# Output projections in two Strassen groups: additions to the accumulators moved, and VectorE's fixed order made longer

## The chip, the cores and the metric

The kernel runs on one core of a Trainium2 chip. The metric is the device time of one execution in microseconds (us), as the median of several executions. The engines are named as in the profile: PE is TensorE (matrix products), DVE VectorE, ACT ScalarE, POOL GpSimd, SP SyncE (which issues DMAs).

## What is computed

A decoder trunk of two layers on one sequence of 1024 tokens with 1024 features, all in float32. Layer 0 mixes tokens by sliding-window attention, layer 1 by a chunked spatial gating unit (SGU); after each comes a gated feed-forward block (FFN) with a short convolution. Each of the four blocks stands between two RMS norms.

```python
for i in range(DEPTH):
    h = rms_norm(x, norm_mix_pre[i])
    h = sliding_window_attention(h, ...) if i % 2 == 0 else chunked_sgu(h, ...)
    x = x + rms_norm(h, norm_mix_post[i])
    h = conv_gated_ffn(rms_norm(x, norm_ffn_pre[i]), ...)
    x = x + rms_norm(h, norm_ffn_post[i])

def conv_gated_ffn(h, w_in, conv_w, conv_b, w_out):
    g, u = jnp.split(h @ w_in, 2, axis=-1)
    ...
    return (jax.nn.gelu(g) * u) @ w_out
```

The change concerns the last product of a block, `... @ w_out`, in three of the four: both FFNs (2816 rows of `w_out`) and the SGU (3072 rows).

## The kernel before

**Products.** A float32 product is made of three passes over rounded operands: each operand is split into a high and a low half (`split`, line 806: a copy on ACT at line 808, then a subtraction on DVE, by the helper at line 602), and PE computes high by high, high by low and low by high (`passes`). A DVE or ACT instruction takes a tile of 128 x 512.

**Output projection.** `out_phase_` (line 911 on) is run three times: FFN of layer 0, SGU, FFN of layer 1. `w_out`'s rows come in chunks of 128: 22 in an FFN, 24 in the SGU. Pairs of chunks are multiplied by Strassen's scheme in Winograd's form, seven products in place of eight, over quarters of the 1024 x 1024 output: accumulators `c[i, j]`, four tiles of 128 x 512 each, i and j from zero (`c[1, 0]` is the lower left quarter). The first group g1 has six pairs (products P1, P2, P6, P5, P7, P3, P4), the second group g2 has n2 pairs, four in an FFN and five in the SGU, in the order Q1, Q2, Q6, Q5, Q3, Q7, Q4. The last two chunks are multiplied directly: `chunk` splits them in Q1 (tiles `ohl`), and `part` adds their products to the same PSUM banks as Q2, Q3, Q7 or Q4 use.

**Steps.** A product has one step for each pair: `prepare` splits its two operands into `osum` tiles, `go` does the product's extra work `what(g)` for this pair and then 12 matmuls (line 880). In the last step of a product, `more` is called for each of its four banks as that is done, and `done` for all four. Steps are numbered through: 0 to 41 are g1; in an FFN Q1 is 42 to 45, Q2 46 to 49, Q6 50 to 53, Q5 54 to 57, Q3 58 to 61, Q7 62 to 65, Q4 66 to 69. In the SGU each has five: Q2 is 47 to 51, Q6 52 to 56, Q4 ends with 76.

**Extra work in g2.** `sums2` (in Q2's steps) does three DVE subtractions on blocks that Q6 and Q5 read, `sums4` (in Q5's) one DVE addition to a block that Q3 reads. `c11` (Q2's `more`; the names of these functions count from one, so it completes the quarter `c[0, 0]`) calls `part`: an addition from the bank to the accumulator on DVE (line 262), the square with its sum on ACT (line 269, output `junk`), a multiplication by the gain on DVE (line 270); line 275 begins the norm. Q1's result is copied to four tiles `u` (the list `ww`). `u2` (Q6's `done`) adds Q6's banks to them and the sums to `c[1, 0]`; `u4` (Q5's `done`) subtracts and adds the result to `c[0, 1]` and `c[1, 1]`. `c12`, `c22` and `c21` complete and normalise the other parts.

**Order.** `run_products` (line 890) writes out the order: step i's `go` comes after the `prepare` of step i + 2, from step 38 on of step i + 3. For steps 0 to 29 (`5 * NPAIR`) DVE takes its instructions in just that order; from there on a scheduler orders DVE's queue, as it does the other engines' throughout. The `osum` tiles come from a pool of eight (`wp`), of which two of the `ohl` pairs take four from Q1 on. The `mm` banks are four; Q1, Q5 and Q7 use them, while Q6 and Q3 use the banks `ob` and `tb`.

Of the kernel before, what the change touches and what calls it, by code (L numbers as in the profile page):

```python
# [37 lines left out]
def trunk_kernel(  # L38
# [113 lines left out]
    def half_of(i):  # L152
        return slice(i * HALF, (i + 1) * HALF)
# [447 lines left out]
    def sub_(out, a, b, eng=None):  # L601
        (eng or nc.vector).tensor_tensor(out=out, in0=a, in1=b, op=ALU.subtract)  # L602

    def add_(out, a, b, eng=None):
        (eng or nc.vector).tensor_tensor(out=out, in0=a, in1=b, op=ALU.add)  # L605
# [182 lines left out]
    NPAIR = 6  # L788
# [100 lines left out]

    def run_products(products):  # L890

        steps = [s for p in products for s in p.steps()]
        n = 0

        def go(i0, i1):
            nonlocal n
            for i in range(i0, i1):
                while n < min(i + AHEAD[i >= 7 * NPAIR - 4] + 1, len(steps)):
                    steps[n][0]()
                    n += 1  # L900
                steps[i][1]()

        with tc.manual_schedule(engines={mybir.EngineType.DVE}):
            go(0, 5 * NPAIR)
        go(5 * NPAIR, len(steps))

    def out_phase(nchunk, ad, w_out, make_sub):
        with tc.tile_pool(name="junkp", bufs=2) as junkp:
            return out_phase_(nchunk, ad, w_out, make_sub, junkp)

    def out_phase_(nchunk, ad, w_out, make_sub, junkp):
# [10 lines left out]
        def w_block(j0):  # L922
            return lambda g, k, i: w_out[tok(j0 + 2 * g + k), half_of(i)]
# [21 lines left out]
        c = {(i, j): [sub.acc[4 * i + t][:, half_of(j)] for t in range(4)] for i in range(2) for j in range(2)}  # L945
# [13 lines left out]
        def add_to(dst):  # L959
            def f(b):  # L960
                for t in range(4):
                    add_(dst[t], b[t], dst[t])
            return f

        def less(dst, src):

            def f(b):
                for t in range(4):
                    sub_(dst[t], b[t], src[t])
            return f  # L970

        def from_(dst, src):

            def f(b):
                for t in range(4):
                    sub_(dst[t], src[t], b[t])
            return f

        def both(*fs):
            def f(b):  # L980
                for x in fs:
                    x(b)
            return f

        def same(p):
            return lambda: p.banks
# [8 lines left out]
        P5 = Product(g1, "P5", four0, both(g1.late, g1.sums4), less(c[0, 1], c[1, 0]))  # L995
        P7 = Product(g1, "P7", four1, None, both(from_(c[1, 1], c[0, 1]), lambda b: load((0, 1))))
        P3 = Product(g1, "P3", four0, None, add_to(c[0, 1]))
# [4 lines left out]
        g2 = Group(n2, [(xnp, "xn")] * 4 + [(work, "work")] * (n2 - 4), w_block(2 * NPAIR))  # L1002
# [5 lines left out]
        def load(parts):  # L1008
            for item in list(todo):
                what, k, i, g, part = item  # L1010
                free = [p for p in parts if spare[p] and p in (part, 2)]
                if not free:
                    continue
                todo.remove(item)
                t = spare[free[0]].pop(0)
                j = 2 * NPAIR + 2 * g + k
                if what == "A":
                    nc.sync.dma_start(out=t, in_=ad[j][:, half_of(i)])
                    g2.A[g][i, k] = t
                else:  # L1020
                    nc.sync.dma_start(out=t, in_=w_out[tok(j), half_of(i)])
                    g2.B[g][k, i] = t
# [24 lines left out]
        ww = []  # L1047
# [7 lines left out]
        def u2(b):  # L1055
            for t in range(4):
                add_(ww[t], b[t], ww[t])
                add_(c[1, 0][t], ww[t], c[1, 0][t])

        def u4(b):  # L1060
            for t in range(4):
                sub_(ww[t], b[t], ww[t])
                add_(c[0, 1][t], ww[t], c[0, 1][t])
                add_(c[1, 1][t], ww[t], c[1, 1][t])

        def c11(t, b):
            part(t, 0, b)
# [14 lines left out]
        Q1 = Product(g2, "P1", four0, both(g2.sums1, chunk), u1)  # L1082
        Q2 = Product(g2, "P2", same(Q1), g2.sums2, more=c11, first=False)
        Q6 = Product(g2, "P6", four1, g2.sums3, u2)
        Q5 = Product(g2, "P5", four0, g2.sums4, u4)
        Q3 = Product(g2, "P3", four1, more=c12)
        Q7 = Product(g2, "P7", four0, None, c22)
        Q4 = Product(g2, "P4", same(Q7), more=c21, first=False)
        run_products(seq + [Q1, Q2, Q6, Q5, Q3, Q7, Q4])
        return sub.h  # L1090

# [376 lines left out]
```

## Time and profile before

| | |
|---|---|
| median of three executions | 2475.07 us (2474.7 to 2475.67) |
| the profiled execution | 2475.61 us, of which span 2473.9 us |
| PE busy | 2414.4 us |
| DVE busy | 1851.3 us |
| ACT busy | 1052.4 us |
| matmuls of line 880 in the chain that ended last | 17% of the span |

The span is the time from the first instruction in the profile to the last; the rest of an execution lies around it. Busy time of PE includes matmuls that run at a lower clock. In a timeline each row is an instruction, or some alike in a row (x4), with its start, its time, its line and in brackets the idle time of the engine just before it and what ended that. One instruction's time overlaps the next one's start a little, so costs are read from start to start.

### The profile page before, as it was taken

How to read it: one execution, taken by the hardware profiler on the slowest of the kernel's cores; microseconds unless marked ns; L12 is line 12 of the kernel's file. 1: busy time of each engine (PE TensorE's matmuls, PEld its weight loads, DVE VectorE, ACT ScalarE, POOL GpSimd, SP SyncE). 2: the span in 40 equal slices, each digit the busy share in tenths (PEclk: the TensorE clock that was granted, in tenths of full speed). 3: DMA queues.
4: the chain of work that ended last, by engine and by line, in shares of the span. 5: the costliest groups of instructions: out<-in, count | busy, mean ns of one | idle time of the engine just before them, and what ended most of it. 6: DMA issues, size and time to landing. Idle time of an engine off the chain costs nothing.

```text
span 2473.9 us, 33879 instructions
## 1 busy us (share of the span) xinstructions
PE 2414.4 (98%) x12488; PEld 2029.6 (82%) x12488; DVE 1851.3 (75%) x3224; ACT 1052.4 (43%) x1957; POOL 341.8 (14%) x442
## 2 busy tenths in 40 slices
PE   9999989999999999999999999999999999999997
PEld 8777778888887787789998888788797888887886
DVE  5766799767767887886667776787887767767877
ACT  4654565333333444443333333444453333334443
POOL 1000010000000111100027777202110000001011
PEclk9999999999999999999999999999999999999999
DMA  7322142222224952433334444974222222238642
GB/s 238 65 47 56 44 154 69 77 87 92 69 94 154 260 156 69 153 107 99 94 97 148 135 141 150 295 220 81 94 95 85 68 94 86 76 103 259 192 86 102
DMA packets 269943, 296.34 MB, mean 120 GB/s; under 512 B 30447, under 2 KB 195665, under 8 KB 269778
## 3 DMA queue, kind: packets, MB, share of 16 engines
q1 hardware_dynamic: 257106, 271.11, 34.2%
q0 software_dynamic: 12672, 23.07, 5.7%
q8 instruction: 98, 1.61, 0.3%
q14 instruction: 67, 0.55, 0.1%
HBM read 211.29 MB, written 65.01 MB: 112 GB/s over the span
## 4 chain that ended last, share of the span: by engine, by line
PE 84%; DVE 10%; DMA 3%; issue 2%; ACT 1%; POOL 0%; SPq 0%; DVEq 0%; POOLq 0%; ACTq 0%
PE mm L748 27%; PE ob L748 11%; PE mm L880 11%; PE mm L148 7%; PE mm L1286 6%; PE ob L880 3%; PE ob L259 3%; PE tb L880 3%; PE ob L1286 2%; DVE osum L602 2%; PE tb L1416 2%; DMA raw<-ad 2%; PE mm L259 1%; DMA raw<-in_ffn_w_out 1%; PE tb L473 1%
## 5 line engine op out<-in xcount | busy, mean ns | idle before, releaser
L748 PE MATMUL mm<-T,wsum 128*128 128x512 f32 x2496 | 597.4, 392 | 5.4 <-ACT wsum L710 4.2
L748 PEld LDWEIGHTS mm<-T,wsum 128*128 128x128 f32 x2496 | 468.3, 189 | 105.8 <-ACT wsum L710 6.0
L880 PE MATMUL mm<-osum 128*128 128x512 f32 x1644 | 390.1, 391 | 8.1 <-ACT osum L808 4.4
L880 PEld LDWEIGHTS mm<-osum 128*128 128x128 f32 x1644 | 306.6, 188 | 76.0 <-DVE osum L602 5.8
L808 ACT CAST osum<-raw 128x512 fp32r<-128x512 f32 x372 | 215.8, 619 | 305.2 <-PE mm L880 103.7
L602 DVE TENSOR_TENSOR osum<-raw,osum 128x512 fp32r<-128x512 f32 x372 | 242.9, 690 | 84.2 <-ACT osum L808 84.0
L748 PE MATMUL ob<-hhi,wsum 128*128 128x512 f32 x864 | 287.3, 393 | 0.1
L710 ACT CAST wsum<-sums 128x512 fp32r<-128x512 f32 x208 | 127.7, 621 | 292.8 <-DVE sums L602 164.1
L1401 POOL TENSOR_SCALAR vn<-vn,mv,rv 128x128 f32<-128x128 f32 x192 | 193.3, 1018 | 73.9 <-DMA vn<-vd 26.2
L602 DVE TENSOR_TENSOR wsum<-sums,wsum 128x512 fp32r<-128x512 f32 x208 | 142.8, 690 | 68.0 <-ACT wsum L710 67.5
L748 PEld LDWEIGHTS ob<-hhi,wsum 128*128 128x128 f32 x864 | 161.7, 188 | 35.7 <-ACT wsum L710 3.4
L748 PE MATMUL ob<-hlo,wsum 128*128 128x512 f32 x432 | 168.7, 390 | 0.0
L710 ACT CAST wsum<-raw 128x512 fp32r<-128x512 f32 x156 | 96.5, 620 | 163.7 <-PE mm L748 140.3
L605 DVE TENSOR_TENSOR pu<-mm,pu 128x512 f32<-128x512 f32 x110 | 75.7, 688 | 105.4 <-PE mm L748 105.3
L880 PE MATMUL ob<-osum 128*128 128x512 f32 x480 | 133.8, 393 | 13.8 <-DVE osum L602 13.8
L148 PE MATMUL mm<-hhi,whi 128*128 128x256 f32 (+1 forms) x416 | 136.0, 329 | 0.7 <-ACT hhi L211 0.7
L148 PE MATMUL mm<-hlo,whi 128*128 128x256 f32 (+1 forms) x416 | 135.7, 327 | 0.0
L148 PE MATMUL mm<-hhi,wlo 128*128 128x256 f32 (+1 forms) x416 | 134.6, 325 | 0.2 <-DVE wlo L125 0.2
L880 PE MATMUL tb<-osum 128*128 128x512 f32 x480 | 132.5, 389 | 0.0
L748 PE MATMUL mm<-hhi,wsum 128*128 128x512 f32 x384 | 126.7, 391 | 0.0
L1116 DVE SCALAR_TENSOR_TENSOR cv<-gs,cw,cv 128x1024 f32<-128x1024 f32 (+1 forms) x100 | 115.7, 1157 | 14.1 <-issue 8.3
L880 PEld LDWEIGHTS ob<-osum 128*128 128x128 f32 x480 | 88.9, 188 | 38.0 <-DVE osum L602 20.2
(257 smaller groups left out, 4526.6 us busy)
## 6 DMA issues: line engine op xcount, KB each, us to landing
raw<-in_ffn_w_in SPq DMA_DIRECT2D x88, 512.0 KB, 4.0
raw<-ad SPq DMA_DIRECT2D x80, 256.0 KB, 5.4
raw<-in_ffn_w_out SPq DMA_DIRECT2D x80, 256.0 KB, 5.7
ad<-cv SPq DMA_DIRECT2D x38, 512.0 KB, 3.2
raw<-in_sgu_w_in SPq DMA_DIRECT2D x28, 512.0 KB, 4.4
xs<-xt SPq DMA_DIRECT2D x24, 512.0 KB, 2.6
vn<-vd SPq DMA_DIRECT2D x48, 256.0 KB, 3.2
ads<-ut SPq DMA_DIRECT2D x24, 512.0 KB, 3.1
```

Of the source, the lines that this page charges most:

```text
L148: nc.tensor.matmul(ps[:, cs], a[:, k, :], b[:, k, cs], start=n == 0, stop=n == 3 * KC - 1)
L259: nc.tensor.matmul(ps, a, b[:, half_of(nh)], start=n == 0 and not begun, stop=n == end, skip_group_check=begun)
L602: (eng or nc.vector).tensor_tensor(out=out, in0=a, in1=b, op=ALU.subtract)
L605: (eng or nc.vector).tensor_tensor(out=out, in0=a, in1=b, op=ALU.add)
L710: nc.scalar.copy(out=t[:, 0], in_=src)
L748: nc.tensor.matmul(bank, x, y, start=first and n == 0, stop=n == 3 * H4 - 1, skip_group_check=True)
L808: nc.scalar.copy(out=t[:, 0], in_=src)
L880: nc.tensor.matmul(self.banks[t], u, v, start=self.first and g == 0 and m == 0, stop=last and self.more is None and m == 2, skip_group_che ...
L1116: nc.vector.scalar_tensor_tensor(out=cv, in0=gs[j][:, k + t0:k + t0 + n], scalar=tap_w(k, j), in1=cv, op0=ALU.mult, op1=ALU.add)
L1286: nc.tensor.matmul(bank[r][:, q * NQ:(q + 1) * NQ], x, y, start=first and q == 0 and m == 0, stop=m == 3 * H4 - 1, skip_group_check=True)
L1401: nc.gpsimd.tensor_scalar(out=vn[:, t, :], in0=vn[:, t, :], scalar1=mv[:, tt, 0:1], scalar2=rv[:, tt:tt + 1], op0=ALU.subtract, op1=ALU.mult)
L1416: nc.tensor.matmul(sv[:, t, :], vn[:, t, :], gws[(j + i) // 3][0], start=True, stop=True)
```

## The change

It does two things. First, `u2` and `u4` keep only the four additions or subtractions on the `u` tiles. What they added to the accumulators, a new function `plus_u(i, j)` does, one tile a step, in the first four steps of a later product: `c[1, 0]` in Q5's (ahead of sums4), `c[0, 1]` in Q3's, `c[1, 1]` in Q7's. Second, DVE's fixed order now reaches to step 61 of an FFN's 70 steps and step 66 of the SGU's 77: all but the last step of Q3, and Q7 and Q4.

```diff
+        fixed = len(steps) - 2 * products[-1].group.n - 1
         with tc.manual_schedule(engines={mybir.EngineType.DVE}):
-            go(0, 5 * NPAIR)
-        go(5 * NPAIR, len(steps))
+            go(0, fixed)
+        go(fixed, len(steps))
...
         def u2(b):
             for t in range(4):
                 add_(ww[t], b[t], ww[t])
-                add_(c[1, 0][t], ww[t], c[1, 0][t])
 
         def u4(b):
             for t in range(4):
                 sub_(ww[t], b[t], ww[t])
-                add_(c[0, 1][t], ww[t], c[0, 1][t])
-                add_(c[1, 1][t], ww[t], c[1, 1][t])
+
+        def plus_u(i, j):
+
+            return lambda t: add_(c[i, j][t], ww[t], c[i, j][t]) if t < 4 else None
...
-        Q5 = Product(g2, "P5", four0, g2.sums4, u4)
-        Q3 = Product(g2, "P3", four1, more=c12)
-        Q7 = Product(g2, "P7", four0, None, c22)
+        Q5 = Product(g2, "P5", four0, both(plus_u(1, 0), g2.sums4), u4)
+        Q3 = Product(g2, "P3", four1, plus_u(0, 1), more=c12)
+        Q7 = Product(g2, "P7", four0, plus_u(1, 1), c22)
```

What this does to the order of the engines' queues is shown for the FFN of layer 0; the numbers in names tell tiles apart. Lines behind 889 are two or three higher in the changed kernel.

**VectorE, from Q2 to Q6.** `acc_7333` to `acc_7336` are the tiles on which c11 works; `osum_8386` and `osum_8389` are the two splits for Q6's first step, `osum_8408` and `osum_8411` for its second. Before:

```order
L602 TENSOR_TENSOR osum_8386<-raw1_7275,osum_8386 128x512
L602 TENSOR_TENSOR osum_8389<-sums_7341,osum_8389 128x512
L262 TENSOR_TENSOR acc_7333<-mm_8256,acc_7333 128x512
L270 TENSOR_TENSOR acc_7333<-acc_7333,gpost_7263 128x512
L275 TENSOR_SCALAR ms_8759<-ss2_8451 128x1
L262 TENSOR_TENSOR acc_7334<-mm_8257,acc_7334 128x512
L262 TENSOR_TENSOR acc_7335<-mm_8258,acc_7335 128x512
L270 TENSOR_TENSOR acc_7334<-acc_7334,gpost_7263 128x512
L275 TENSOR_SCALAR ms_8790<-ss2_8465 128x1
L602 TENSOR_TENSOR osum_8408<-raw1_7275,osum_8408 128x512
L602 TENSOR_TENSOR osum_8411<-sums_7342,osum_8411 128x512
```

In the changed kernel, where the three subtractions of sums2 for Q2's last step and the beginning of c11 stand (`osum_8429` and `osum_8432` are the splits for Q6's third step):

```order
L602 TENSOR_TENSOR osum_8429<-raw1_7275,osum_8429 128x512
L602 TENSOR_TENSOR osum_8432<-sums_7343,osum_8432 128x512
L602 TENSOR_TENSOR sums_7344<-raw1_7277 128x512
L602 TENSOR_TENSOR raw1_7277<-raw1_7275,raw1_7277 128x512
L602 TENSOR_TENSOR raw1_7275<-sums_7344,raw1_7275 128x512
L262 TENSOR_TENSOR acc_7333<-mm_8255,acc_7333 128x512
L270 TENSOR_TENSOR acc_7333<-acc_7333,gpost_7263 128x512
```

and c11's end, with the splits for Q6's last step (`osum_8495`, `osum_8498`) and for Q5's first (`osum_8518`, `osum_8521`):

```order
L270 TENSOR_TENSOR acc_7335<-acc_7335,gpost_7263 128x512
L262 TENSOR_TENSOR acc_7336<-mm_8258,acc_7336 128x512
L275 TENSOR_SCALAR ms_8829<-ss2_8478 128x1
L270 TENSOR_TENSOR acc_7336<-acc_7336,gpost_7263 128x512
L602 TENSOR_TENSOR osum_8495<-raw1_7275,osum_8495 128x512
L602 TENSOR_TENSOR osum_8498<-sums_7344,osum_8498 128x512
L602 TENSOR_TENSOR osum_8518<-sums_7341,osum_8518 128x512
L602 TENSOR_TENSOR osum_8521<-raw1_7275,osum_8521 128x512
```

Before, c11's instructions stood around the splits for Q6's second step, and sums2's subtractions were far ahead (with P4 and Q1). Now they stand behind the splits for Q6's third step and all subtractions, and ahead of those for its last.

**ScalarE, at the same place.** The squares of c11's tiles are the four lines 269. Before (the copies are for Q6's steps, two each, and Q5's first, `osum_8519` and `osum_8522`):

```order
L269 ACTIVATE junk_8443,ss2_8451<-acc_7333 128x512
L269 ACTIVATE junk_8457,ss2_8465<-acc_7334 128x512
L808 CAST osum_8408<-raw1_7275 128x512
L808 CAST osum_8411<-sums_7342 128x512
L269 ACTIVATE junk_8471,ss2_8479<-acc_7335 128x512
L269 ACTIVATE junk_8485,ss2_8493<-acc_7336 128x512
L808 CAST osum_8430<-raw1_7275 128x512
L808 CAST osum_8433<-sums_7343 128x512
L808 CAST osum_8496<-raw1_7275 128x512
L808 CAST osum_8499<-sums_7344 128x512
L808 CAST osum_8519<-sums_7341 128x512
L808 CAST osum_8522<-raw1_7275 128x512
```

In the changed kernel (`osum_8518` and `osum_8521` are for Q5's first step):

```order
L808 CAST osum_8429<-raw1_7275 128x512
L808 CAST osum_8432<-sums_7343 128x512
L808 CAST osum_8495<-raw1_7275 128x512
L808 CAST osum_8498<-sums_7344 128x512
L808 CAST osum_8518<-sums_7341 128x512
L808 CAST osum_8521<-raw1_7275 128x512
L269 ACTIVATE junk_8442,ss2_8450<-acc_7333 128x512
L269 ACTIVATE junk_8456,ss2_8464<-acc_7334 128x512
L269 ACTIVATE junk_8470,ss2_8478<-acc_7335 128x512
L269 ACTIVATE junk_8484,ss2_8492<-acc_7336 128x512
L808 CAST osum_8537<-sums_7342 128x512
```

The squares moved from among the copies for Q6's first steps to behind those for Q5's first.

**VectorE, from Q5 to Q3.** `acc_7337` to `acc_7340` hold the lower rows' accumulators, `acc_7333` to `acc_7336` the upper ones'; `osum_8628` and `osum_8631` are splits for Q3's second step, `osum_8608` and `osum_8611` for its first. Before:

```order
L602 TENSOR_TENSOR osum_8608<-raw1_7276,osum_8608 128x512
L602 TENSOR_TENSOR osum_8611<-raw1_7276,osum_8611 128x512
L602 TENSOR_TENSOR u_8358<-mm_8590,u_8358 128x512
L602 TENSOR_TENSOR u_8358<-mm_8591,u_8358 128x512
L602 TENSOR_TENSOR u_8359<-mm_8592,u_8359 128x512
L602 TENSOR_TENSOR u_8359<-mm_8593,u_8359 128x512
L605 TENSOR_TENSOR acc_7333<-u_8358,acc_7333 128x512
L605 TENSOR_TENSOR acc_7337<-u_8358,acc_7337 128x512
L605 TENSOR_TENSOR acc_7334<-u_8358,acc_7334 128x512
L602 TENSOR_TENSOR osum_8628<-raw1_7276,osum_8628 128x512
L605 TENSOR_TENSOR acc_7338<-u_8358,acc_7338 128x512
L602 TENSOR_TENSOR osum_8631<-raw1_7276,osum_8631 128x512
```

In the changed kernel (`raw1_7276<-raw1_7276,raw1_7275` is a sums4 addition, `osum_8646` and `osum_8649` are for Q3's third step, `osum_8671` and `osum_8674` for its last):

```order
L605 TENSOR_TENSOR acc_7339<-u_8358,acc_7339 128x512
L605 TENSOR_TENSOR raw1_7276<-raw1_7276,raw1_7275 128x512
L602 TENSOR_TENSOR osum_8646<-raw1_7276,osum_8646 128x512
L602 TENSOR_TENSOR osum_8649<-raw1_7276,osum_8649 128x512
L605 TENSOR_TENSOR acc_7340<-u_8358,acc_7340 128x512
L605 TENSOR_TENSOR raw1_7276<-raw1_7276,raw1_7275 128x512
L602 TENSOR_TENSOR u_8357<-mm_8585,u_8357 128x512
L602 TENSOR_TENSOR u_8357<-mm_8586,u_8357 128x512
L602 TENSOR_TENSOR u_8358<-mm_8587,u_8358 128x512
L602 TENSOR_TENSOR u_8358<-mm_8588,u_8358 128x512
L605 TENSOR_TENSOR acc_7337<-u_8357,acc_7337 128x512
L602 TENSOR_TENSOR osum_8671<-raw1_7276,osum_8671 128x512
```

Of u4, the four subtractions and one addition now stand between the splits for Q3's third and last step; the sums4 additions, done long before in Q1 and Q2 until now, stand one ahead of each pair of splits.

## Rows read from the trace of the kernel before

**Rows 1.** Page, part 1: busy time and share of each engine.
```profile
PE 2414.4 (98%) x12488; PEld 2029.6 (82%) x12488; DVE 1851.3 (75%) x3224; ACT 1052.4 (43%) x1957; POOL 341.8 (14%) x442
```

**Rows 2.** Page, part 4: chain that ended last, share of the span by engine.
```profile
PE 84%; DVE 10%; DMA 3%; issue 2%; ACT 1%; POOL 0%; SPq 0%; DVEq 0%; POOLq 0%; ACTq 0%
```

**Rows 3.** PE's waits, whole program: total us, times, longest us.
```profile
PE ob L880 <- DVE osum L602: 13.8, 15, 1.7
...
PE mm L880 <- DVE osum L602: 2.5, 6, 0.6
```

**Rows 4.** PE timeline, Q5 and Q3: start, us; in brackets idle before.
```profile
956.83 7.55 PE L880 MATMUL mm<-osum 128*128 128x512 f32 x32 [0.50 <-DVE osum L602]
...
969.71 1.19 PE L880 MATMUL ob<-osum 128*128 128x512 f32 x4 [1.70 <-DVE osum L602]
...
973.32 1.20 PE L880 MATMUL ob<-osum 128*128 128x512 f32 x4 [0.60 <-DVE osum L602]
```

**Rows 5.** DVE timeline, Q5's end, first FFN phase (same columns).
```profile
963.56 2.48 DVE L602 TENSOR_TENSOR u<-mm,u 128x512 f32<-128x512 f32 x4
965.96 1.89 DVE L605 TENSOR_TENSOR acc<-u,acc 128x512 f32<-128x512 f32 x3
...
969.56 2.50 DVE L605 TENSOR_TENSOR acc<-u,acc 128x512 f32<-128x512 f32 x4
971.97 2.50 DVE L602 TENSOR_TENSOR osum<-raw,osum 128x512 fp32r<-128x512 f32 x4
```

**Rows 6.** PE timeline, Q6's last step, first FFN phase.
```profile
949.82 0.61 PE L880 MATMUL ob<-osum 128*128 128x512 f32 x2
...
950.73 1.07 PE L880 MATMUL ob<-osum 128*128 128x512 f32 x4
```

**Rows 7.** ACT timeline, Q2 and Q6, first FFN phase.
```profile
937.21 0.63 ACT L269 ACTIVATE junk<-acc 128x512 f32<-128x512 f32 x1 [2.64 <-DVE acc L262]
...
944.58 0.62 ACT L808 CAST osum<-raw 128x512 fp32r<-128x512 f32 x1 [0.56 <-PE tb L880]
...
950.02 0.62 ACT L808 CAST osum<-sums 128x512 fp32r<-128x512 f32 x1 [1.52 <-PE tb L880]
950.55 0.61 ACT L808 CAST osum<-raw 128x512 fp32r<-128x512 f32 x1
```

**Rows 8.** DVE timeline, Q2, first FFN phase.
```profile
932.94 1.28 DVE L602 TENSOR_TENSOR osum<-raw,osum 128x512 fp32r<-128x512 f32 x2
...
936.42 0.69 DVE L262 TENSOR_TENSOR acc<-mm,acc 128x512 f32<-128x512 f32 x1 [0.39 <-PE mm L259]
937.96 0.69 DVE L270 TENSOR_TENSOR acc<-acc,gpost 128x512 f32<-128x512 f32 x1 [0.85 <-ACT junk L269]
...
941.32 0.68 DVE L602 TENSOR_TENSOR osum<-raw,osum 128x512 fp32r<-128x512 f32 x1
```

**Rows 9.** DVE and PE timelines, Q6, SGU phase.
```profile
1711.58 0.69 DVE L602 TENSOR_TENSOR osum<-sums,osum 128x512 fp32r<-128x512 f32 x1
...
1716.46 1.07 PE L880 MATMUL ob<-osum 128*128 128x512 f32 x4
```

**Rows 10.** PE timeline around the longest idle time, 1057 to 1072.
```profile
1062.59 1.08 PE L210 MATMUL tb<-ident,xn 128*128 128x128 f32 x4 [2.89 <-DVE t L602]
...
1065.22 0.63 PE L1434 MATMUL tb<-wlo,hhi 128*128 128x512 f32 x1
...
1069.06 0.45 PE L1434 MATMUL tb<-wlo,hhi 128*128 128x512 f32 x1
```

**Rows 11.** Windows: us, then five engines' busy time, granted clock, DMA share, GB/s.
```profile
967.50:970.00 2.50, 0.80 (x4) 0.38 (x3) 2.50 (x5) 0.78 (x2) 0.00 (x0) 1.00 0.00 0
1060.00:1062.50 2.50, 0.00 (x0) 0.00 (x0) 2.50 (x7) 0.48 (x1) 0.00 (x0) 0.97 0.28 105
1062.50:1065.00 2.50, 1.46 (x5) 1.09 (x6) 2.50 (x3) 1.23 (x3) 0.00 (x0) 0.50 0.00 0
1065.00:1067.50 2.50, 2.50 (x7) 1.93 (x7) 2.50 (x5) 1.04 (x1) 0.00 (x0) 0.50 0.00 0
```

## The prediction

> **What bounds the kernel now.** I read the page first. TensorE (PE) is busy for 2414.4 us, VectorE (DVE) for 1851.3 [rows 1], and the chain that ended last is 84% PE [rows 2]. So the product passes set the time, and a change to VectorE's work can only act through the moments in which PE waits. The list of PE's waits gives those that belong to the output projections (line 880): 13.8 us for second halves of the splits ahead of products that go to the `ob` and `tb` banks, 2.5 us for those of `mm` products [rows 3]. Listed for the three places where the second group runs, the change's own target is the same each time: PE waits 0.50 us in Q5 and 1.70 and 0.60 us in Q3 [rows 4], 2.8 us a phase, **8.4 us in all**. VectorE's timeline says why: with Q5's last product at hand it does u4's four subtractions and eight additions, with only two splits among them, and Q3's next four splits start at 971.97 [rows 5]. That is the most that the change can win directly.
>
> The second thing to see is how tight the splits are elsewhere. A step has 12 matmuls; four of them take 0.91 us (949.82 to 950.73, [rows 6]), the step 2.72. Two operand tiles of a step may be overwritten only when an older step has ended: ScalarE's copies for a split start about 0.2 us after one, at 944.58 and 950.02, both after a wait for PE [rows 7]. So a split is made at most two steps ahead, and a VectorE queue that is late by more than that stops PE.
>
> **The change part by part.** No instruction is added or removed: the twelve additions of u2 and u4 are the same twelve, 0.60 us apart on VectorE (four in 2.40 us, [rows 5]). Two things move.
>
> *The additions.* In Q5 each step now has on VectorE, in this order: one addition to `c[1, 0]`, one sums4 addition, then the two splits of the step three ahead, which need that sums4. From one sums4 to the next this is a serial path: sums4 0.69, ScalarE's first copy 0.62 [rows 7], two splits and one addition at 0.60, some 0.05 for each of the three hand-overs: about 3.25 us, against 2.72 for PE's step. Followed step by step it stops PE by 0.1, 0.55, 0.5 and 0.5 us, and u4's four subtractions with one addition, now fixed ahead of the splits for Q3's last step, by 1.2: 2.9 us where 2.8 are taken away. **A wash in the two FFN phases.** In the SGU phase, with five steps to a product, the splits have one step more of slack, and I get 1.1 for 2.8: **-1.7 us**.
>
> *The fixed order.* This part touches more than the additions. Before, VectorE's order was fixed only up to step 30, and the scheduler did the subtractions of sums2 long before Q2; the function c11's work at the end of Q2 (line 262, then line 270, on four tiles) ran between the splits, the first at 936.42 [rows 8]. Now everything up to Q3 is taken in the order of the text, in which a step's preparation comes three steps ahead and sums2 in the step itself: on VectorE all twelve subtractions of sums2 now come before c11's first addition, and the splits of Q6's last step come behind all of c11.
>
> Worked out for the first FFN phase: the splits for Q2's last step end at 934.14 (two from 932.94, [rows 8]). Then three subtractions (1.80 us) and two splits alternate; the third pair's copies start as now at 944.58, when their tiles come free [rows 7], 0.62 and two splits later it is 946.45, and the last three subtractions end at 948.25. Only then does c11's first addition start. Each of the four tiles goes from line 262 on VectorE to the square on ScalarE and back to line 270. That is 1.54 us (936.42 to 937.96, [rows 8]), and 2.14 with the step to the next tile. For the first tile it is 3.6: on ScalarE its square now stands behind the two copies for Q5's first step, which can't start before 950.02 [rows 7] and end at 951.07. So line 270 comes at 951.82, the three other tiles take 3 x 2.14 = 6.42, and the last line 270 is at 958.24. Behind it stand the two splits of Q6's last step, done at 960.13. PE has its first four matmuls of that step without them, and the first four of Q5, which now stand next; it needs the splits at 950.73 + 0.91 = 951.64 [rows 6] and goes on at 960.19. **A new wait of 8.55 us**, where the trace shows none. Four lone matmuls of Q5 fall into it, as the c11 additions give their banks free.
>
> The second FFN phase has the same order and the same waits: again 8.55. In the SGU phase the splits before c11 end about 1712.2 (1711.58 + 0.60, [rows 9]), sums2's last three subtractions at 1714.0, four tiles take 1.54 + 6.42, so line 270 is last at 1721.96, the two splits end at 1723.85, and PE, which wants them at 1716.46 [rows 9], waits 7.45 us.
>
> *What the wait does to PE's clock.* Where PE stood still for 2.89 us at 1060 [rows 10], the granted clock was 0.50 in the two stretches that followed [rows 11], which is 1.2 GHz, the lower of the two levels. Ten matmuls, from 1065.22 to 1069.06, were 0.427 us apart [rows 10] where 0.227 is usual: 2.0 us lost. Where PE stood still for 1.70 us ahead of 969.71, the granted clock stayed at 1.00 [rows 4, 11]. The new wait is some three times the longer of the two, so I take 2.0 us for each of the three phases, and keep 0 as the other end, since four matmuls lie in the wait and none lies in the one at 1060. The Trainium skill, "TensorE: Matmul & The Clock Gate", section "HAM oscillation — how this bites in real kernels", tells of a kernel whose waits between groups of matmuls made each group begin slow again, so that the price is paid at every wait and not once. By that rule the three waits cost 6 us more, and by the row at 969.71, which disagrees for a shorter wait, nothing.
>
> **The sum.** FFN phases 2 x (8.55 + 0.07) = 17.2; SGU 7.45 - 1.7 = 5.75; together 23.0. The clock adds 3 x 2.0 = 6.0: **+29.0 us**. The profiled execution took 2475.61 us, 0.54 above the median of 2475.07; 2475.61 + 29.0 - 0.5 gives **2504 us**. Q7 and Q4 keep the scheduler's order; the work there is the same, with four additions more in Q7's steps and four fewer before them, and I cost it at nothing. The waits ahead of their products are short, and VectorE has no longer to do than before; if the cover fails, it is the last rival below.
>
> **Rivals.** (a) *The same wait, and the clock holds*, because the matmuls of Q5 in it keep PE at its higher level: +23, 2498 us. For it: those four matmuls; against: one each two microseconds.
> (b) *The wait is only about half as long.* If ScalarE's squares are not held behind the copies (3.6 to 1.54 us for the first tile) and the last three subtractions are done while VectorE waits elsewhere (1.8), the FFN phases lose 8.55 - 3.85 = 4.7 each, the SGU phase some 4: +13.5, 2489 us. For it: VectorE waits for ScalarE at several places of Q2 now; against: both engines take their queues as listed, and ScalarE's list has the copies first.
> (c) *Faster: the change does what its additions suggest, and no new wait arises.* The three waits of each phase go, 8.4 us: 2475.07 - 8.4 = 2467 us. It decides itself at one point: the two splits of Q6's last step must end before 951.64. For it: splits now have no u4 additions ahead of them, and VectorE was idle a quarter of the span. Against: they stand behind c11's eight instructions, with a square between the two of each tile, and the first of these can't start before 948.25.
> (d) *No change:* the new waits in Q5 and Q6 and the old ones cancel, or the fixed order takes up only idle time: 2475 us. Against it speaks the size of the new wait.
> (e) *More:* the additions now in Q7's steps come late and delay the norms; four of 0.60 us in each phase, on top of the forecast: +7, 2511 us.
>
> **How the numbers follow.** Forecast (2500 to 2509) 0.50; (a) 0.20; (b) 0.12; (c) 0.09; (d) 0.04; (e) 0.05. The likeliest is 2504. Eight in ten are held by the forecast, (a) and the upper part of (b), with half of (e): 2485 to 2511 us. A difference of 0.2% (5 us) is about what can be told from no change here: faster 0.09, same 0.04, slower 0.87.
>
> **What would show it.** Right: in the changed trace the list of PE's waits has one wait of 7 to 9 us in Q6's last step of each phase, put down to VectorE's split or to the banks that line 262 frees; VectorE's timeline there shows lines 262 and 270 about 2.1 us apart, idle between them for line 269; the granted clock falls just behind it. In Q5 and Q3 PE's waits are several of about half a microsecond in place of 1.70 and 0.60. Wrong: no PE wait over 2 us in Q6 makes it (c) or (d), one of 4 to 5 us (b), a granted clock of 1.00 behind it (a).

## The result, and the profile after

The changed kernel takes **2508.99 us** (median; 2508.44 to 2510.2), the kernel before 2475.37 beside it: a ratio of 1.0137, with an interval from 1.0124 to 1.015. That is 33.6 us more, where 29.0 were forecast, and inside the range, near its upper end. The profiled execution has a span of 2506.7 us (2473.9 before).

The page's first part (busy time, its share of the span) answers to [rows 1]:

```profile
PE 2430.5 (97%) x12488; PEld 2036.7 (81%) x12488; DVE 1855.6 (74%) x3224; ACT 1052.6 (42%) x1957; POOL 341.3 (14%) x442
```

VectorE and ScalarE work as long as before. PE is busy for 16 us more with as many instructions, in part at a lower clock; the rest of the 32.8 us is waiting. The list of PE's waits, whole program (us in total, times, longest), has more in the first entry of [rows 3], and an entry in which `mm` products wait for line 262, which was not there:

```profile
PE ob L880 <- DVE osum L602: 20.2, 15, 7.5
PE mm L880 <- DVE acc L262: 5.9, 4, 1.6
```

Most of what is new lies at the end of Q6. PE's timeline of the first FFN phase (start, time, what, in brackets the idle time before), against [rows 4 and 6], with the `ob` matmuls of Q3 at its end:

```profile
951.53 0.50 PE L880 MATMUL mm<-osum 128*128 128x512 f32 x1
953.48 0.61 PE L880 MATMUL mm<-osum 128*128 128x512 f32 x1 [1.45 <-DVE acc L262]
...
957.70 0.79 PE L880 MATMUL mm<-osum 128*128 128x512 f32 x1 [1.35 <-DVE ms L275]
960.45 2.07 PE L880 MATMUL ob<-osum 128*128 128x512 f32 x4 [1.95 <-DVE osum L602]
...
964.00 10.14 PE L880 MATMUL mm<-osum 128*128 128x512 f32 x44
...
980.60 0.74 PE L880 MATMUL ob<-osum 128*128 128x512 f32 x2 [0.22 <-ACT osum L808]
...
986.80 0.73 PE L880 MATMUL ob<-osum 128*128 128x512 f32 x2 [0.67 <-DVE osum L602]
```

The four lone matmuls of Q5 from 951.53 on come one by one as line 262 frees their banks, with some 1.4 us of idle time before each, and the second half of Q6's last step, which was due at 951.9, starts at 960.45. VectorE's timeline of the same stretch answers to [rows 8]:

```profile
934.38 0.68 DVE L602 TENSOR_TENSOR sums<-raw 128x512 f32<-128x512 f32 x1
935.10 0.69 DVE L602 TENSOR_TENSOR raw<-raw,raw 128x512 f32<-128x512 f32 x1
...
948.84 0.68 DVE L262 TENSOR_TENSOR acc<-mm,acc 128x512 f32<-128x512 f32 x1
952.13 0.69 DVE L270 TENSOR_TENSOR acc<-acc,gpost 128x512 f32<-128x512 f32 x1 [2.61 <-ACT junk L269]
...
954.21 0.69 DVE L270 TENSOR_TENSOR acc<-acc,gpost 128x512 f32<-128x512 f32 x1 [0.73 <-ACT junk L269]
...
958.50 0.69 DVE L270 TENSOR_TENSOR acc<-acc,gpost 128x512 f32<-128x512 f32 x1 [0.79 <-ACT junk L269]
959.11 0.68 DVE L602 TENSOR_TENSOR osum<-raw,osum 128x512 fp32r<-128x512 f32 x1
959.71 1.29 DVE L602 TENSOR_TENSOR osum<-sums,osum 128x512 fp32r<-128x512 f32 x2
```

The splits of Q2's last step end at 934.38, and sums2's first subtraction starts then; c11's first addition comes at 948.84, behind the last. Each line 270 is 2.1 us behind the one before it, the last at 958.50, and behind it the two splits that PE waits for. ScalarE's timeline shows why the first tile takes 3.3 us from line 262 to line 270; its square (line 269) stands behind two copies that wait until 950.34 for their tiles, against [rows 7]:

```profile
950.34 0.62 ACT L808 CAST osum<-sums 128x512 fp32r<-128x512 f32 x1 [0.17 <-PE tb L880]
950.86 0.61 ACT L808 CAST osum<-raw 128x512 fp32r<-128x512 f32 x1
951.38 0.63 ACT L269 ACTIVATE junk<-acc 128x512 f32<-128x512 f32 x1
```

The windows (length, busy time of PE, PEld, DVE, ACT and POOL, then the granted clock) answer to [rows 11]:

```profile
950.00:952.50 2.50, 1.92 (x7) 0.86 (x5) 0.37 (x1) 1.94 (x5) 0.00 (x0) 1.00 0.02 7
952.50:955.00 2.50, 0.61 (x1) 0.19 (x1) 1.77 (x5) 0.72 (x2) 0.00 (x0) 0.74 0.00 0
955.00:957.50 2.50, 0.80 (x1) 0.29 (x1) 1.71 (x4) 0.72 (x2) 0.00 (x0) 0.50 0.00 0
...
960.00:962.50 2.50, 2.05 (x5) 1.67 (x6) 1.66 (x4) 0.00 (x0) 0.00 (x0) 0.50 0.00 0
962.50:965.00 2.50, 2.50 (x10) 1.97 (x9) 0.15 (x1) 0.80 (x2) 0.00 (x0) 0.71 0.00 0
```

The granted clock falls between 952.5 and 955, is 0.50 from there on, and comes back between 962.5 and 965. In the SGU phase, where Q6 has five steps, the wait lies in the fourth, and no lone matmuls fall into it: it is one wait of 7.50 us, and the eight matmuls behind it (1739.22 to 1742.54) again take longer than the 1.8 us that they take at full clock:

```profile
1739.22 2.07 PE L880 MATMUL ob<-osum 128*128 128x512 f32 x4 [7.50 <-DVE osum L602]
...
1742.54 0.62 PE L880 MATMUL ob<-osum 128*128 128x512 f32 x2
```

Going by matmuls that both traces have, the time came in at these places:

| place | before, us | after, us | later by, us |
|---|---|---|---|
| Q6's first matmul, first FFN phase | 941.66 | 941.92 | 0.3 |
| the transpose behind PE's longest idle time, after that phase | 1062.59 | 1076.64 | 14.1 |
| Q1 in the SGU phase | 1693.64 | 1708.74 | 15.1 |
| the last direct products of the SGU phase (`tb`, twelve) | 1790.19 | 1812.12 | 21.9 |
| g1 in the second FFN phase (`ob`, six) | 2352.78 | 2376.08 | 23.3 |
| the last direct products of that phase | 2454.99 | 2487.95 | 33.0 |

So the three phases cost 13.8, 6.8 and 9.7 us, 30.3 in all, and 2.7 came in outside them.

### The profile page after: what moved, and what is told of

Same layout as the page of the kernel before. It is cut to its first block, busy times and chain, and to the rows that moved or that the text cites. A ratio compares the mean times of both kernels' runs of the same rounds, so it can differ in the third digit from the quotient of the medians.

```text
span 2506.7 us, 33941 instructions
## 1 busy us (share of the span) xinstructions
PE 2430.5 (97%) x12488; PEld 2036.7 (81%) x12488; DVE 1855.6 (74%) x3224; ACT 1052.6 (42%) x1957; POOL 341.3 (14%) x442
## 4 chain that ended last, share of the span: by engine, by line
PE 85%; DVE 10%; ACT 2%; issue 2%; DMA 1%; POOL 0%; SPq 0%; DVEq 0%; POOLq 0%; ACTq 0%
PE mm L748 27%; PE mm L880 12%; PE ob L748 11%; PE mm L148 7%; PE mm L1289 6%; PE ob L259 4%; PE ob L880 3%; PE tb L880 3%; PE ob L1289 2%; DVE osum L602 2%; PE tb L1419 2%; PE mm L524 1%; PE mm L259 1%; PE tb L473 1%; PE mm L514 1%
```

## The experiments

The theory was that of the prediction: the fixed order puts c11's round trips between VectorE and ScalarE ahead of the splits for Q6's fourth step. Rival A blames the moved additions, B sums2's subtractions ahead of c11, C says that Q7 and Q4 take back what Q5 and Q3 gain, D that something else than the clock slows the matmuls behind the wait. Ratios are to the kernel before on the same chip; the change has 1.0137.

### One part of the change at a time

*The additions alone*: the changed kernel with

```diff
-        fixed = len(steps) - 2 * products[-1].group.n - 1
+        fixed = 5 * NPAIR
```

> The additions of u2 and u4 are moved as in the change, VectorE's fixed order stays as before (to step 30). Theory (the loss is made by the fixed order at the end of Q2, the moved additions cost nothing): the scheduler puts the moved additions back where they stood, so nothing changes; 2475 us, between 2472 and 2479, Q5 and Q3 wait 0.50, 1.70 and 0.60 us as before. Rival A (the additions in Q5's, Q3's and Q7's steps are what costs, by the serial path from sums4 to sums4): 2490 us or more.

Measured: 2476.72 us, ratio 1.0001 (0.9991 to 1.001). PE's timeline has the three waits of [rows 4] to the hundredth:

```profile
957.33 7.59 PE L880 MATMUL mm<-osum 128*128 128x512 f32 x32 [0.50 <-DVE osum L602]
...
970.25 1.19 PE L880 MATMUL ob<-osum 128*128 128x512 f32 x4 [1.70 <-DVE osum L602]
...
973.86 1.21 PE L880 MATMUL ob<-osum 128*128 128x512 f32 x4 [0.60 <-DVE osum L602]
```

The order of VectorE's queue in this stretch is that of the kernel before: u4's twelve instructions stand together again, with two splits among them. So moving them in the text does nothing unless the order is fixed, and rival A is not the loss.

*The order alone*: the kernel before with

```diff
-            go(0, 5 * NPAIR)
-        go(5 * NPAIR, len(steps))
+            go(0, len(steps) - 2 * products[-1].group.n - 1)
+        go(len(steps) - 2 * products[-1].group.n - 1, len(steps))
```

> VectorE's fixed order is made longer as in the change, the additions stay inside u2 and u4 as before. Theory: the wait of about 8 us in Q6's last step and the lower clock behind it are there in all three phases, and u4's twelve instructions in one piece, now fixed ahead of the splits for Q3's last step, add 2 to 3 us a phase to what the change has: 2516 us, between 2508 and 2522. Rival A (the moved additions cost, the order doesn't): 2475 to 2482 us.

Measured: 2524.12 us, ratio 1.0192 (1.0177 to 1.0207). The direction and the wait in Q6 are as expected, the size is not: 47 us more than the kernel before, where 41 were expected, and above the range. PE's timeline has, beyond Q6's wait, one in Q5 where u2's eight instructions are ahead of the splits, and one behind u4's twelve (5.27 us in the SGU phase):

```profile
973.81 2.12 PE L880 MATMUL mm<-osum 128*128 128x512 f32 x8 [2.21 <-DVE osum L602]
...
991.32 1.22 PE L880 MATMUL ob<-osum 128*128 128x512 f32 x2 [2.03 <-DVE osum L602]
```

By the totals that is some 5 us a phase more than in the change, not 2 to 3. With the order fixed, then, the spread of the additions is worth about 14 us (1.0192 against 1.0137): the change's first part helps against a loss that its second part brings.

*The order free up to Q5, fixed from there*: the changed kernel with

```diff
         with tc.manual_schedule(engines={mybir.EngineType.DVE}):
-            go(0, fixed)
+            go(0, 5 * NPAIR)
+        q5 = len(steps) - 4 * products[-1].group.n
+        go(5 * NPAIR, q5)
+        with tc.manual_schedule(engines={mybir.EngineType.DVE}):
+            go(q5, fixed)
         go(fixed, len(steps))
```

> The changed kernel, but the scheduler orders VectorE from step 30 to the end of Q6 as before; fixed again only from Q5's first step to the change's end in Q3. Theory: the wait in Q6's last step and the fall of the clock behind it are gone, Q5 and Q3 wait about as long as before in several smaller waits, Q7 and Q4 cost 1 us in all: 2477 us, between 2472 and 2482. Rival A (the serial path of additions and splits in Q5 and Q3 is the loss): 2495 us or more.

Measured: 2475.14 us, ratio 0.9994 (0.9985 to 1.0003). In PE's timeline Q6's last step and all of Q5 run without a wait, and Q3 has small ones, this the longest:

```profile
951.99 11.04 PE L880 MATMUL mm<-osum 128*128 128x512 f32 x48
...
974.83 0.73 PE L880 MATMUL ob<-osum 128*128 128x512 f32 x2 [0.67 <-DVE osum L602]
```

All of the loss is gone, and what is left of the change, the spread additions in a fixed order, is worth nothing that can be measured.

### What in the fixed order it is

*c11's gains later*: `part` may hold back its last instruction, and Q6's steps run what was held:

```diff
-                nc.vector.tensor_tensor(out=y[:, half_of(nh)], in0=acc, in1=self.gpost[:, half_of(nh)], op=ALU.mult)
+                gain = lambda: nc.vector.tensor_tensor(out=y[:, half_of(nh)], in0=acc, in1=self.gpost[:, half_of(nh)],
+                                                       op=ALU.mult)
+                gain() if hold is None else hold.append(gain)
...
-            part(t, 0, b)
+            part(t, 0, b, hold=held)
...
-        Q6 = Product(g2, "P6", four1, g2.sums3, u2)
+        Q6 = Product(g2, "P6", four1, both(g2.sums3, gain), u2)
```

> The changed kernel with one thing moved: c11's four multiplications by the gain (line 270) come one in each of Q6's steps and no longer right behind each tile's square, so the four additions of line 262 stand together. Theory (the wait in Q6 is the four round trips to ScalarE): from the end of sums2 at 948.84 four additions take 2.4 us and two splits 1.9, so PE waits 1.3 us in place of 8.6 in the first FFN phase, 2.1 in place of 7.5 in the SGU phase, and the clock stays up: 2483 us, between 2478 and 2488. Rival B (the wait comes from sums2's subtractions standing ahead of c11, not from the round trips): at most 3 us less a phase, over 2498 us.

Measured: 2482.75 us, ratio 1.0025 (1.0015 to 1.0034). VectorE's timeline has the four additions in a row and the splits right behind them (lines are two higher in this kernel):

```profile
949.29 2.48 DVE L262 TENSOR_TENSOR acc<-mm,acc 128x512 f32<-128x512 f32 x4
951.68 0.68 DVE L604 TENSOR_TENSOR osum<-raw,osum 128x512 fp32r<-128x512 f32 x1
952.28 0.69 DVE L604 TENSOR_TENSOR osum<-sums,osum 128x512 fp32r<-128x512 f32 x1
```

PE goes from Q5's first four matmuls, which are no longer apart, to the second half of Q6's last step without a listed wait:

```profile
951.98 1.20 PE L882 MATMUL mm<-osum 128*128 128x512 f32 x4
953.02 1.20 PE L882 MATMUL ob<-osum 128*128 128x512 f32 x4
```

By start times PE loses 0.8 us there in this phase, where the change loses 8.55 and 1.7 more by the lower clock. The four multiplications alone are 2.4 us of work; the rest is mainly VectorE's idle time in the round trips, 4.9 us as listed in the change (2.61, 0.73 and twice 0.79). Four instructions a phase, moved by some microseconds, take back four fifths of the loss (1.0025 of 1.0137), with sums2 where it was. Rival B falls; its own part is the next run.

*sums2's subtractions early*: the changed kernel with

```diff
             self.plus(t[:, 1], B[0, 0])
+
+        def diffs(self, g):
+            A, t = self.A[g], self.temps[g]
             sub_(t[:, 0], A[1, 0], A[1, 1])
...
-        Q1 = Product(g2, "P1", four0, both(g2.sums1, chunk), u1)
+        Q1 = Product(g2, "P1", four0, both(g2.sums1, chunk, g2.diffs), u1)
```

> The changed kernel with one thing moved: sums2's three subtractions stand in Q1's steps (its DMA addition stays in Q2's), so that c11 comes right behind the splits for Q6's third step; the round trips of c11's tiles to ScalarE stay. Theory (the round trips are the larger part): in the first FFN phase c11 starts about 2.1 us earlier, the first square is no longer held, and PE still waits about 5.3 us in Q6 (8.6 in the change), in the SGU phase about 5.5 (7.5), with the clock still falling: 2500 us, between 2493 and 2505. Rival B (sums2's subtractions ahead of c11 are the cause): under 2487 us.

Measured: 2504.9 us, ratio 1.0117 (1.0103 to 1.013); at the upper end of what was expected. c11 starts at 947.60, and the round trips take 9.1 us (10.3 in the change, where the first square is held), so that the splits start at 956.71:

```profile
947.60 0.69 DVE L262 TENSOR_TENSOR acc<-mm,acc 128x512 f32<-128x512 f32 x1
...
956.71 0.69 DVE L602 TENSOR_TENSOR osum<-raw,osum 128x512 fp32r<-128x512 f32 x1
```

PE's timeline has a wait of 0.52 us at the end of Q2, where VectorE has the last of the moved subtractions ahead of the splits, and still 2.25 us ahead of Q6's second half, behind lone matmuls as in the change:

```profile
936.31 0.73 PE L883 MATMUL mm<-osum 128*128 128x512 f32 x2 [0.52 <-DVE osum L602]
...
958.05 2.08 PE L883 MATMUL ob<-osum 128*128 128x512 f32 x4 [2.25 <-DVE osum L602]
```

The second half of Q6's last step was due at 952.8 and starts at 958.05: 5.25 us, as expected, and 3.3 less than in the change. Two things take most of that back: PE loses 1.2 us by start times in the wait at Q2's end and one just before it, and from the 44 matmuls of Q5 to Q3's first it takes 11.0 us (961.63 to 972.63) in place of 10.1, the first of them still at a granted clock of 0.50. Alone, this part is small, and its interval overlaps that of the change.

### What the lower clock costs

*Zeros in the wait*: the changed kernel with 26 matmuls that keep PE at work while it waits. They multiply by a tile of zeros, so they add nothing to their bank.

```diff
+                            if self.name == "P6" and self.group.n < NPAIR and g == 3 and t == 3 and m == 0:
+                                for k in range(26):
+                                    nc.tensor.matmul(self.banks[3], zeros[-1], cb[:, 0], start=False, stop=False,
+                                                     skip_group_check=True)
...
```

> The changed kernel with PE kept at work in the new wait: between the first four matmuls of Q6's fourth step and what follows them, 26 matmuls with a weight of zeros that add nothing to a bank, 5.9 us at 0.227 us each, less than the wait (8.55 us in the FFN phases, 7.5 in the SGU phase), so that the wait's end is where VectorE's splits put it, as in the change. Theory (the fall of the clock costs 1.7 to 2.0 us a phase beside the wait itself): the granted clock stays at 1.00 behind the wait, the eight matmuls after it take 1.8 us in place of 3.5, and the kernel is 5 us faster than the change though it does more: ratio to the kernel before 1.0116 (1.010 to 1.0125), where the change has 1.0137. Rival D (the matmuls after the wait are slow for another reason, or the clock falls all the same): 1.0135 or more.

Measured: 2502.17 us, ratio 1.011 (1.0093 to 1.0127). PE's timeline has the zeros (line 884), a wait of 2.23 us that is left, and the eight matmuls behind it in 1.95 us, where the change took 3.55:

```profile
949.33 6.06 PE L884 MATMUL tb<-osum,zero 128*128 128x512 f32 x26
...
958.53 1.20 PE L880 MATMUL ob<-osum 128*128 128x512 f32 x4 [2.23 <-DVE osum L602]
959.56 1.08 PE L880 MATMUL tb<-osum 128*128 128x512 f32 x4
960.48 10.13 PE L880 MATMUL mm<-osum 128*128 128x512 f32 x44
```

The granted clock of the windows there:

```profile
957.50:960.00 2.50, 1.47 (x6) 1.24 (x7) 2.24 (x5) 0.00 (x0) 0.00 (x0) 1.00 0.00 0
960.00:962.50 2.50, 2.50 (x12) 2.06 (x11) 1.17 (x2) 1.15 (x3) 0.00 (x0) 1.00 0.00 0
```

The wait ends where VectorE's splits put it, as in the change, and the time behind it is back. The kernel does 78 matmuls more, and by the ratios it is 0.27% faster than the change (6.7 us; 5 were expected); the two intervals just overlap, so the size is better read from the timelines: 1.6 us in this phase, 1.4 in the SGU phase and 1.6 in the second FFN phase, 4.6 in all. The lower clock was a part of the loss beside the wait, and rival D falls.

### A version that beats both

*Order free up to Q5, and sums4 out of Q5*: as the third run, and sums4 in Q6's steps, where the scheduler may do it early.

```diff
-        Q6 = Product(g2, "P6", four1, g2.sums3, u2)
-        Q5 = Product(g2, "P5", four0, both(plus_u(1, 0), g2.sums4), u4)
+        Q6 = Product(g2, "P6", four1, both(g2.sums3, g2.sums4), u2)
+        Q5 = Product(g2, "P5", four0, plus_u(1, 0), u4)
```

> VectorE's order free from step 30 to the end of Q6 as in the earlier experiment, fixed in Q5 and Q3, and sums4 in Q6's steps, where the scheduler may do it early. Theory: the serial path from sums4 to sums4 is gone, so the small waits of Q5 and Q3 that were left (about 1.5 us a phase) go too: ratio to the kernel before 0.997 (0.9955 to 0.9985), some 5 us less than without the move. Rival C (Q7 and Q4 take back whatever Q5 and Q3 gain): ratio 0.999 or more.

Measured: 2470.53 us, ratio **0.9976** (0.9967 to 0.9984), 0.18% under the run without the move. In PE's timeline Q5 and Q3 have one wait left in the first FFN phase, of 0.33 us, ahead of Q7's first matmuls, which stand in Q3's last step:

```profile
972.37 1.19 PE L880 MATMUL mm<-osum 128*128 128x512 f32 x4 [0.33 <-ACT osum L808]
```

On VectorE the splits for Q3's first steps were 3.26 us apart without the move (961.55, 964.82, 968.08) and are 2.72 apart with it (960.95, 963.67, 966.39), which is PE's own step. So the serial path from sums4 to sums4, with which the prediction explained the small waits of Q5 and Q3, is what made them. From Q6's end to Q7's start the three phases are now 3.1, 2.6 and 3.1 us shorter than in the kernel before; some 6 of these 8.8 us are left in the kernel's time. Q7 and Q4 of the first phase take 1.2 back; the rest was not followed up.

*All of it in a fixed order*: the changed kernel with the gains later, sums2's subtractions in Q1 and sums4 in Q6's steps, the edits as above.

> The changed kernel with the fixed order kept to Q3, and three things moved in it: c11's multiplications by the gain one in each of Q6's steps, sums2's subtractions in Q1's steps, sums4 in Q6's steps. Theory: no wait in Q6, no serial path in Q5 and Q3, so of the kernel before the 2.8 us a phase go (8.4), and Q7 and Q4, as in the change, take back 1 to 4: 7 us less than the kernel before, ratio 0.997 (0.9955 to 0.9985). Rival A (additions spread over the steps cost as such): no faster than the kernel before.

Measured: 2473.25 us, ratio 0.9988 (0.9979 to 0.9997): in the right direction, but just outside the range that was expected. A fixed order can be as good as the scheduler's when no round trip stands in it; the wait of 0.5 us at the end of Q2 is there as in the run with sums2's subtractions early.

*The additions to `c[1, 1]` in Q3*, none in Q7, with the order free up to Q5 and sums4 in Q6's steps. ("The one before" is here the run that first had these two, with 2470.53 us.)

```diff
-        Q3 = Product(g2, "P3", four1, plus_u(0, 1), more=c12)
-        Q7 = Product(g2, "P7", four0, plus_u(1, 1), c22)
+        Q3 = Product(g2, "P3", four1, both(plus_u(0, 1), plus_u(1, 1)), more=c12)
+        Q7 = Product(g2, "P7", four0, None, c22)
```

> As the one before, with the additions to c[1, 1] in Q3's steps beside those to c[0, 1] and none in Q7's. Theory: VectorE has 2.4 us of work for each step of 2.72 in Q3, still no wait there, and Q7 and Q4 wait no longer than in the kernel before: 1 to 3 us less than the run before, ratio 0.996 (0.9945 to 0.998). Rival C (Q7's additions aren't what delays Q7 and Q4): the same as the run before within 1 us.

Measured: 2471.95 us, ratio 0.9985 (0.9976 to 0.9994). A miss: no gain over the 0.9976 of that run, whose interval it overlaps. Without additions in Q7, Q7 and Q4 of the first phase take longer, not shorter (4.0 us more than in the kernel before; 1.2 more with them), so these additions are not what delays them.

## Why the prediction was right, and where it was off

**The wait in Q6's last step: right, to the size.** Forecast 8.55 us for an FFN phase; from 951.9, when PE was due, to 960.45 it is 8.55. Forecast 7.45 for the SGU; listed 7.50, and 7.66 from when PE was due (1731.56) to its start (1739.22). The step that carried it was to read the new order of two queues together. One price in it was too low: the subtractions of sums2 start 0.72 us apart (934.38, 935.10), not 0.60, and c11 started a third of a microsecond later than worked out; the held square took that up. One sign was put badly: in the FFN phases the wait is listed in four pieces, none over 2 us, because of the lone matmuls that the prediction itself placed there; by "no PE wait over 2 us in Q6" these phases would have counted against it.

**The lower clock: right.** Forecast 2.0 us a phase, with 0 as the other end. The eight matmuls behind the wait took 3.55 us in place of 1.81 in the FFN phase (1.7 us more), 3.32 in the SGU (1.5 more), 3.58 in the second FFN phase (1.8 more), and the run with zeros gives it back. The four lone matmuls did not keep the clock up, so rival (a) fell. The rule that the prediction took from the Trainium skill ("TensorE: Matmul & The Clock Gate", section "HAM oscillation — how this bites in real kernels") holds here: the price was paid at each of the three waits, also where single matmuls broke the wait up. That waits near 2 us pay it only at times is told in the last section.

**Q5 and Q3: called a wash, and the order of size is right.** In the change Q3's steps start with listed waits of 0.2 us and one of 0.67, and more of the loss is spread between matmuls, as the serial path of 3.26 us a step (973.53 to 976.79 on VectorE) against PE's 2.72 makes it. That it was this path is shown by the run that takes sums4 out of it. By start times an FFN phase loses 0.1, then 0.54 at each of three steps, and 0.95 where 1.2 was forecast, 2.7 in all, near the 2.9 forecast. The old waits, read in the same way, were worth 3.3 us, not the listed 2.8. So Q5 and Q3 gave 0.7 us back in each FFN phase, where 0.07 were to be lost, and 2.3 in the SGU phase, where 1.7 were forecast.

**The sum: 29.0 forecast, 33.6 measured (32.8 in the span).** Read between like-numbered matmuls of line 880 in the two traces (Q2's last, the eighth after Q6's, the seventh after Q3's, Q4's last), and over all three phases:

| part | forecast, us | measured, us |
|---|---|---|
| Q6's wait and the lower clock | 30.6 | 30.1 |
| Q5 and Q3 | -1.6 | -3.7 |
| Q7 and Q4 | 0 | 3.9 |
| outside the phases | no term | 2.7 |

That the total came so near is in part luck: Q5 and Q3 gave back 2.1 us more than forecast, which hides half of what Q7 and Q4 cost. The term that was mis-sized most is "Q7 and Q4 ... I cost it at nothing". In the first FFN phase, forecast at 10.6 and measured at 13.8, they take 4.2 us more than before, and PE waits at these two places of them, in place of 1.13 and 0.19 us:

```profile
1010.50 0.66 PE L210 MATMUL tb<-ident,xn 128*128 128x128 f32 x4 [2.55 <-DVE hlo L212]
...
1021.87 3.47 PE L880 MATMUL mm<-osum 128*128 128x512 f32 x14 [1.09 <-DVE osum L602]
```

In the SGU and the second FFN phase Q7 and Q4 are 0.1 and 0.2 us shorter than before, so "nothing" held there. In the first phase VectorE comes late to c12: its first addition (line 262, 991.49) starts 4.1 us after the direct products that it waits for begin on PE (987.37), in the kernel before 1.6 us (978.21 and 976.65). In the changed kernel splits and moved additions fill VectorE's time ahead of it without a break. The runs narrow it down: Q7 and Q4 of this phase cost nothing where the scheduler orders the moved additions, 1.2 us in the two runs with sums4 in Q6's steps and the additions left in Q7, 3.0 to 4.2 in all others that fix the order to Q3, the one without additions in Q7 included. So it seems to go with VectorE's work in Q5 and Q3 and not with the additions in Q7; which instructions decide it is not shown. The other part is 2.7 us outside the phases: 1.4 of it came in between the SGU phase and the second FFN phase, where the clock fell in a place that the change doesn't touch (last section); 1.0 came in between the first phase and the SGU's, 0.3 ahead of the first, and these were not followed up.

**The rivals.** (c), the faster case, was decided at the point that the prediction named: the splits came at 959.11, not before 951.64. (b) took the first square as not held back; in the FFN phases it was held (3.3 us from line 262 to line 270), in the SGU phase it was not (1.53), as the forecast had it. (d) fell with the size of the wait. (e) has its place right, late norms in Q7 and Q4 of the first phase, but not its cause, as the run without additions in Q7 shows.

## What to carry to other kernels

A fixed order is a promise about every instruction in the range, not just about those for which it was made: before fixing one, list what else lies between the same two points, and look for pairs on one engine with another engine's work between them. Such a round trip costs its whole latency in a fixed queue (2.1 us a tile here, of which VectorE is idle for 0.8), and taking the two halves apart, all first halves and then other work and then the second halves, cost a few lines and gave back four fifths of the loss. And when a scheduler reorders freely, moving a statement in the text may move nothing: compare the queues first.

## What was not expected of the hardware

**The same wait, and the clock falls once and not the other time.** At the start of the second FFN phase's output projection PE waits for ScalarE in both kernels, 1.90 us in the one before, with a granted clock of 1.00 after it:

```profile
2237.77 0.74 PE L880 MATMUL mm<-osum 128*128 128x512 f32 x2 [1.90 <-ACT osum L808]
```

and 1.99 us in the changed one:

```profile
2259.49 0.74 PE L880 MATMUL mm<-osum 128*128 128x512 f32 x2 [1.99 <-ACT osum L808]
```

where two windows, of the kernel before and then of the changed one, differ:

```profile
2240.00:2242.50 2.50, 2.50 (x13) 2.06 (x12) 1.18 (x2) 0.62 (x1) 0.00 (x0) 1.00 1.05 401
```

```profile
2262.00:2264.50 2.50, 2.50 (x8) 1.93 (x7) 0.00 (x0) 0.00 (x0) 0.00 (x0) 0.51 1.05 400
```

In the changed kernel the matmuls there are 0.43 us apart, and from the end of the wait PE needs 8.59 us for what takes 6.97 in the kernel before: 1.6 us lost, at a place that both kernels share. The other runs have nearly the same wait there, 1.9 to 2.5 us in ten of the eleven traces, and in six of these ten the clock falls behind it; a wait of 2.22 us let it stand, and one of 1.99 did not. In comparing two kernels within a few microseconds such a place is part of the difference, though neither edit made it.

**VectorE's instructions are 0.60 us apart, or 0.72.** The three 128 x 512 subtractions of sums2 start 0.72 to 0.73 us apart (934.38, 935.10, 935.83). The second overwrites a block that the first reads; the third reads what the first wrote and overwrites a block that the second reads. Two splits of the same shape that share no tile start 0.60 apart (959.11 and 959.71). The run with the order alone has both kinds in a row in u2: the addition to the accumulator reads the `u` tile that the instruction just before it wrote, and starts 0.72 behind it (967.16, 967.88); the next instruction, on other tiles, starts 0.61 behind that (968.49).
